# Branch A's attention values: two heads side by side as unsplit fp32 products of 64 columns, instead of split fp32r products of one head

## The chip, the cores and the metric

The kernel runs on one core of a Trainium2 chip. The metric is the device time of one execution in microseconds; a kernel is timed in several runs and the median is given. One execution was also taken by the hardware profiler: its page, its trace and the views of it are what this document reads. In them PE is TensorE's matmul stream, PEld its weight loads, DVE VectorE, ACT ScalarE, POOL GpSimd and SP SyncE, which issues the DMAs.

## What is computed

One encoder layer on two groups of 1024 rows of 1024 channels ("prompt" and "sample"), with the same weights. Branch A is grouped-query attention, and its last product is what the change edits:

```python
def gqa_attention(q, k, v):          # q: 8 heads of 64, k and v: 2 heads of 64
    s = jnp.einsum('bqgrd,bkgd->bgrqk', qblk, k).astype(jnp.float32) * scale
    p = jax.nn.softmax(s, axis=-1).astype(v.dtype)
    return jnp.einsum('bgrqk,bkgd->bqgrd', p, v)
```

Branch B is differential attention (4 heads, two softmax maps each, values of 128). Around them: one input projection to 5376 columns, gates, two branch projections, an output projection and a residual. All of it is in fp32.

## The kernel before

The kernel goes through the two groups one after the other. For each, the input projection is done by generators (`kva_gen`, `qa_gen`, `qkb_gen`, `vb_gen`, `z_gen`), each yielding after a few matmuls, and attention is a generator of steps too. `weave` draws from the streams in shares set by tables (`ATT_W`, `Z_SHARE`), and the framework then orders each engine's instructions by its own plan of the timeline, attention with higher priority. So on PE, products of the projections stand between those of attention. SP issues all DMAs in order.

Most products split their operands: a value x is kept as a rounded part xh (type fp32r) and the rest xl, and a product is the sum of two or three fp32r products.

Attention is cut into units of 256 queries. In branch A a unit is one head; there are 32 units per group, in two phases (the first and the second four q heads). A unit has two score steps (`scores`, `softmax_unit`): four products of 512 columns into a PSUM bank (L709, L710), the row maximum on DVE (L711), the exponential on ACT (L712). `flip` turns the probabilities: a block transpose on DVE (L745) and four DMAs into the tile q (L750). After that comes the values part, `a_values`:

- `pT_pieces` takes a quarter of the transposed probabilities at a time, ACT copies its rounded part to `hi` (L758), and DVE subtracts (L759), which leaves the low part in q.
- For each of 8 blocks of 128 keys PE makes two fp32r products of 256 columns: v times hi (L770), v times the low part (L771). The stationary operand has 128 columns: 64 of v's rounded part and 64 of its low part, so that the two halves of the accumulator hold two sums.
- ACT copies one half (L786), DVE adds the other (L787), a DMA stores 64 rows (L791).

Branch B's values (`b_values`, L810) are unsplit already: v and the probabilities in plain fp32, one product per block of keys with 128 stationary columns (the flag `WHOLE` is set for both pairs of heads). Each such product appears in the trace as two records. In the gates for the residual (L435) and at the start (L300) stand fp32 products with 2 stationary columns, and L889 transposes a tile of 64 columns. L497 and L679 are the products of the input projection (256 and 512 columns wide).

`attention` puts the steps of all units in one list, sorted by a number: unit n's score steps at n to n + 1, its values from n + `BEHIND` on.

Of the kernel before, what the change touches and what calls it, by code (L numbers as in the profile page):

```python
# [64 lines left out]
BEHIND = 1.4  # L65
AHEAD = 100
PV_LAG = 2

WHOLE = (True, True)
# [21 lines left out]
def kernel(ctx: ExitStack, tc: tile.TileContext, t: dict):  # L91
# [8 lines left out]
    qpool = ent(tc.tile_pool(name="qpool", bufs=2))  # L100
    tpool = ent(tc.tile_pool(name="tpool", bufs=2))
# [481 lines left out]
    def kva_gen(ht, out):  # L583
        w = kva_w.pop()[0] if kva_w else load_w(w_cols(w_in, (C_KA, 256)))
        k = v2(utile())
        va = utile().rearrange("p (n k d) -> p n k d", n=NTT, k=2)
# [58 lines left out]
    def vb_gen(ht, out, pr):  # L645
        w = load_w(w_cols(w_in, (C_VB + pr * 256, 256)))
        if WHOLE[pr]:
            v = utile().bitcast(F32).rearrange("p (n h e) -> p n h e", n=NTT, h=2)
            out[2 * pr], out[2 * pr + 1] = v[:, :, 0], v[:, :, 1]
        else:  # L650
            vs = [utile().rearrange("p (n s e) -> p n s e", n=NTT, s=2) for _ in range(2)]
            out[2 * pr], out[2 * pr + 1] = vs
        for tt in range(NTT):
            ps = yield from proj_tt(ht, w, tt)
            if WHOLE[pr]:
                nc.scalar.activation(v[:, tt].rearrange("p h e -> p (h e)"), ps, AF.Copy)
                yield 1
                continue
            for i in range(2):
                vp = ps[:, i * P : (i + 1) * P]  # L660
                nc.scalar.activation(vs[i][:, tt, 0, :], vp, AF.Copy)
                nc.vector.tensor_tensor(
                    out=vs[i][:, tt, 1, :], in0=vp, in1=vs[i][:, tt, 0, :].bitcast(F32), op=ALU.subtract
                )
            yield 1
# [51 lines left out]
    def scores(u, i):  # L717

        nm_ = len(u["q"])
        t, m = i // nm_, i % nm_  # L720
        qt = u["pr"] * 2 + t
        if "sw" not in u:
            u["sw"] = swapped(u)
        pt = ptile()
        su = u["su"][:, qt : qt + 1] if m == 0 else tiny.tile([P, 1], F32, tag="su", name=nm("su"))
        softmax_unit(u["q"][m][:, qt * P : (qt + 1) * P], u["sw"][:, m, t * P : (t + 1) * P], u["k"][m], pt, su)
        if m == 0:
# [8 lines left out]
        return t if m == nm_ - 1 else None  # L736

    def flip(u, t):


        pt = u[t][0]
        if len(u[t]) > 1:
            _, p1, f = u[t]
            nc.vector.scalar_tensor_tensor(out=pt, in0=p1, scalar=f, in1=pt, op0=ALU.mult, op1=ALU.add)
        nc.vector.transpose(pt, pt)  # L745
        if t == 0:
            u["pT"] = pair(F32R)
        dst = u["pT"].bitcast(F32).rearrange("p (i t f) -> p i t f", i=4, t=2)
        for i in range(4):
            dma(dst[:, i, t], pt[i * 32 : i * 32 + 32])  # L750

    def pT_pieces(u):

        pT = u["pT"].rearrange("p (q c b) -> p c q b", q=8, c=8)
        for cc in range(4):
            tl = pT[:, cc * 2 : cc * 2 + 2]
            th = tpool.tile([P, 2, 8, 32], F32R, tag="hi", name=nm("hi"), bufs=3)
            nc.scalar.activation(th, tl.bitcast(F32), AF.Copy)  # L758
            nc.vector.tensor_tensor(out=tl, in0=tl.bitcast(F32), in1=th.bitcast(F32), op=ALU.subtract)  # L759
            yield cc, th, tl  # L760

    def a_values(u):
        acc = ps_a.tile([P, 512], F32, tag="a", name=nm("a"))[:, :256]
        ready = []

        def pv(cc, th, tl):
            for c in range(2):
                k = cc * 2 + c
                lt = u["v"](k)
                nc.tensor.matmul(acc, lt, th[:, c, :], start=(k == 0), stop=False)  # L770
                nc.tensor.matmul(acc, lt, tl[:, c, :], start=False, stop=(k == 7))  # L771

        for piece in pT_pieces(u):
            ready.append(piece)
            if len(ready) > PV_LAG:
                pv(*ready.pop(0))
            yield 1
        while len(ready) > 1:
            pv(*ready.pop(0))
            yield 1  # L780
        pv(*ready.pop())
        tmp = mtile("at", [P, 256], bufs=1)
        o = mtile("oo", [P, 256])
        j = u["j"]
        a, b = (slice(0, 64), slice(64, 128)) if j % 2 == 0 else (slice(64, 128), slice(0, 64))
        nc.scalar.activation(tmp[a], acc[b], AF.Copy)  # L786
        nc.vector.tensor_tensor(  # L787
            out=query_order(o[a]), in0=piece_order(acc[a]), in1=piece_order(tmp[a]), op=ALU.add
        )
        pr = u["pr"]  # L790
        dma(u["od"][pr // 2][a, (pr % 2) * 256 : (pr % 2 + 1) * 256], o[a])  # L791
        yield 1

    def b_values(u):
        acc = ps_a.tile([P, 512], F32, tag="a", name=nm("a"))[:, :256]
        ready = []
        def pv(cc, th, tl):
            for c in range(2):
                k = cc * 2 + c
                for s, rt in ((0, th), (0, tl), (1, th)):  # L800
                    nc.tensor.matmul(
                        acc, u["v"][:, k, s, :], rt[:, c, :],
                        start=(k == 0 and s == 0 and rt is th), stop=(k == 7 and s == 1),
                    )

        if WHOLE[u["h"] // 2]:
            pT = u["pT"].bitcast(F32).rearrange("p (q c b) -> p c q b", q=8, c=8)
            yield 1
            for k in range(NCH):
                nc.tensor.matmul(acc, u["v"][:, k], pT[:, k], start=(k == 0), stop=(k == 7))  # L810
                if k % 2:
                    yield 1
        else:
            for piece in pT_pieces(u):
                ready.append(piece)
                if len(ready) > PV_LAG:
                    pv(*ready.pop(0))
                yield 1
            while len(ready) > 1:
                pv(*ready.pop(0))  # L820
                yield 1
            pv(*ready.pop())
# [20 lines left out]
    def attention(units):  # L843
# [11 lines left out]
        for at, ph, n, i, qk in steps:  # L855
# [4 lines left out]
            with tc.high_priority(offset=AHEAD):  # L860
# [12 lines left out]
                if t is not None:  # L873
                    late.append(lambda u=live[n], t=t: flip(u, t))
                    if t == (0 if ph < 2 else 0) and n + 1 < len(units) and units[n + 1][2]():
                        live[n + 1] = units[n + 1][1]()
                        late.append(lambda u=live[n + 1]: u.update(sw=swapped(u)))
# [138 lines left out]
    def units_of(st):  # L1016

        def a_unit(half, i, pr):
            j = half * 4 + i
            kv = j // 4  # L1020
            return {
                "q": [st["qa"][half][i % 2][:, i // 2]], "k": [st["ka"][:, kv]],
                "v": (lambda k: st["va"][:, k, kv, :]),
                "pr": pr, "j": j, "od": st["od"][j // 2], "su": st["suA"][:, j],
# [14 lines left out]
        for half in range(2):  # L1039
            units += [  # L1040
                (half, lambda a=(half, i, pr): a_unit(*a), lambda a=("qa", half, pr): there(*a))
                for i in (0, 2, 1, 3) for pr in range(4)
# [29 lines left out]
    for g in range(2):  # L1072
# [11 lines left out]
        def phase(k, *fs, more=()):  # L1084
            n_att = 16 * (6 + PV_LAG) if k < 2 else 4 * (9 + PV_LAG)
# [96 lines left out]
```

## Time and profile before

| | |
|---|---|
| runs (3): median, lowest, highest | 1982.26, 1980.13, 1987.66 us |
| the profiled execution, its span on the core | 1985.5 us |
| PE busy, records | 1908.6 us (96%), 10466 |
| DVE, ACT, POOL busy | 67%, 51%, 38% |
| branch A's products L770 + L771, records | 512 + 512 |
| branch A's attention runs in (us from the start) | about 150 to 550 and 1150 to 1560 |

A row of a group gives line, engine, operation, what is written from what, the shape (stationary rows*columns, then partitions x moving columns), the number, busy time and mean length of one in ns, then the engine's idle time just before and what ended it. A row of the timeline gives start, length over all, line and how many. Lengths of matmuls overlap, since the next starts before the last has ended: what one costs the stream is the distance of starts or ends.

### The profile page before, as it was taken

The numbers are of one execution on the slowest core, as the hardware profiler recorded it, in microseconds if no ns is written. First come the engines' busy times: TensorE is split into PE (matmuls) and PEld (weight loads), VectorE is DVE, ScalarE is ACT, GpSimd is POOL, SyncE is SP. The second block draws the span as 40 slices with busy tenths as digits, with TensorE's granted clock in tenths as the row PEclk, the third lists the DMA queues.
The fourth block names the chain that finished last, engine by engine and source line by source line (L and its number), as shares of the span: only waits on it lengthen the run. The fifth ranks groups of instructions, "written<-read, shape, count | busy, mean of one in ns | idle before, by whom it ended". The sixth has DMA issues, their size and how long they took to land.

```text
span 1985.5 us, 30670 instructions
## 1 busy us (share of the span) xinstructions
PE 1908.6 (96%) x10466; PEld 1627.8 (82%) x10466; DVE 1330.8 (67%) x1906; ACT 1009.9 (51%) x1939; POOL 758.1 (38%) x1008
## 2 busy tenths in 40 slices
PE   8889999999999998999999899999999999999999
PEld 3878888888878994778888787888887888877887
DVE  4558877777877577547465877677788845665641
ACT  4435655665654444754323565556655534566310
POOL 2374612453446252221235464134445626422110
PEclk9899999999999999999999999999999999999999
DMA  8124556555553345865641455565654333567532
GB/s 310 33 80 126 155 152 169 152 166 154 133 153 102 101 120 173 257 227 167 222 149 35 140 144 145 149 164 144 184 137 137 106 97 99 156 212 245 174 101 75
DMA packets 269531, 295.11 MB, mean 149 GB/s; under 512 B 35776, under 2 KB 218176, under 8 KB 269376
## 3 DMA queue, kind: packets, MB, share of 16 engines
q1 hardware_dynamic: 269376, 293.15, 49.7%
q8 instruction: 84, 1.38, 0.3%
q14 instruction: 71, 0.58, 0.1%
HBM read 133.59 MB, written 42.01 MB: 88 GB/s over the span
## 4 chain that ended last, share of the span: by engine, by line
PE 68%; DMA 8%; DVE 8%; ACT 5%; SPq 4%; issue 3%; POOL 3%; ACTq 0%; POOLq 0%; DVEq 0%
PE f L497 16%; PE f L679 16%; PE f L950 6%; PE f L979 5%; PE s L709 4%; PE a L810 4%; PE s L710 4%; PE s L979 4%; DMA q<-p 3%; SPq L750 3%; PE s L950 2%; DVE q L759 2%; PE a L771 2%; PE a L770 2%; DVE m L711 2%
## 5 line engine op out<-in xcount | busy, mean ns | idle before, releaser
L679 PE MATMUL f<-u,w 128*128 128x512 f32 x2232 | 582.3, 398 | 0.1
L497 PE MATMUL f<-w,u 128*128 128x256 f32 x3456 | 487.0, 286 | 2.2 <-ACT ev L685 1.4
L497 PEld LDWEIGHTS f<-w,u 128*128 128x128 f32 x3456 | 459.5, 192 | 22.4 <-ACT ev L685 1.8
L679 PEld LDWEIGHTS f<-u,w 128*128 128x128 f32 x2232 | 408.8, 190 | 77.3 <-POOL w L181 0.8
L181 POOL TENSOR_TENSOR w<-st,w 128x512 fp32r<-128x512 f32 x168 | 230.3, 1390 | 439.9 <-ACT w L179 375.1
L712 ACT ACTIVATE p<-s,m 128x1024 f32<-128x1024 f32 x256 | 284.4, 1111 | 206.3 <-DVE m L711 111.3
L711 DVE TENSOR_REDUCE m<-s 128x1 f32<-128x1024 f32 x256 | 310.0, 1216 | 51.3 <-PE s L710 48.7
L745 DVE STREAM_TRANSPOSE p<-p 128x1024 f32<-128x1024 f32 x192 | 238.2, 1241 | 99.2 <-ACT p L712 86.5
L759 DVE TENSOR_TENSOR q<-q,hi 128x512 fp32r<-128x512 f32 x256 | 198.3, 792 | 60.6 <-ACT hi L758 58.6
L515 POOL TENSOR_TENSOR rs<-ss,nhalf 128x4 f32<-128x4 f32 (+1 forms) x112 | 112.8, 1007 | 322.8 <-DVE ss L514 284.0
L758 ACT ACTIVATE hi<-q 128x512 fp32r<-128x512 f32 x256 | 153.8, 625 | 104.1 <-DMA q<-p 55.4
L710 PE MATMUL s<-u,sw 128*128 128x512 f32 x512 | 206.7, 404 | 0.0
L179 ACT ACTIVATE w<-st 128x512 fp32r<-128x512 f32 x196 | 113.9, 625 | 97.2 <-DMA st<-in_w_in_dram 46.0
L950 PE MATMUL f<-u,w 128*128 128x512 f32 x552 | 133.4, 395 | 5.1 <-ACT ev L685 4.4
L770 PE MATMUL a<-hi,u 128*128 128x256 f32 x512 | 132.5, 285 | 2.1 <-DVE oo L787 2.1
L771 PE MATMUL a<-q,u 128*128 128x256 f32 x512 | 129.8, 286 | 1.2 <-DVE q L759 1.2
L810 PE MATMUL a<-q,u 128*128 128x256 f32 x512 | 128.3, 390 | 1.9 <-DVE oo L826 1.5
L950 PEld LDWEIGHTS f<-u,w 128*128 128x128 f32 x552 | 103.9, 190 | 27.2 <-ACT ev L685 4.7
L709 PE MATMUL s<-u 128*128 128x512 f32 x256 | 110.9, 433 | 15.1 <-ACT p L712 15.1
L810 PEld LDWEIGHTS a<-q,u 128*128 128x128 f32 x512 | 97.8, 196 | 17.5 <-DVE oo L826 1.6
L709 PE MATMUL s<-u,u 128*128 128x512 f32 x256 | 103.6, 405 | 8.3 <-ACT p L712 7.7
L710 PEld LDWEIGHTS s<-u,sw 128*128 128x128 f32 x512 | 98.4, 192 | 15.5
(175 smaller groups left out, 2562.1 us busy)
## 6 DMA issues: line engine op xcount, KB each, us to landing
q<-p SPq DMA_DIRECT2D x768, 128.0 KB, 2.6
st<-in_w_in_dram SPq DMA_DIRECT2D x132, 256.0 KB, 3.0
zd<-ev SPq DMA_DIRECT2D x96, 256.0 KB, 2.2
sw<-u SPq DMA_DIRECT2D x256, 64.0 KB, 2.1
p<-zd SPq DMA_DIRECT2D x64, 256.0 KB, 3.2
u<-in_w_ada_dram SPq DMA_DIRECT2D x8, 1024.0 KB, 10.4
st<-in_w_in_dram SPq DMA_DIRECT2D x64, 128.0 KB, 2.7
st<-in_w_out_dram SPq DMA_DIRECT2D x32, 256.0 KB, 2.9
```

What stands on the lines that cost most here:

```text
L181: e.tensor_tensor(out=wl, in0=st, in1=wh.bitcast(F32), op=ALU.subtract)
L497: nc.tensor.matmul(ps, lt[c][:, sl], w[:, c, wi, :], start=(k == 0), stop=(k == 23))
L679: nc.tensor.matmul(ps, w[:, c, wi, e * P : (e + 1) * P], rt[c], start=(k == 0), stop=(k == 23),)
L709: nc.tensor.matmul(s[:, sl], q, k[:, sl], start=True, stop=False)
L710: nc.tensor.matmul(s[:, sl], sw, k[:, sl], start=False, stop=True)
L711: nc.vector.tensor_reduce(out=m, in_=s, axis=AX.X, op=ALU.max, negate=True)
L712: nc.scalar.activation(pt.rearrange("p (j c a) -> p j c a", j=4, c=8), s.rearrange("p (c a j) -> p j c a", c=8, j=4), AF.Exp, bias=m, accu ...
L745: nc.vector.transpose(pt, pt)
L759: nc.vector.tensor_tensor(out=tl, in0=tl.bitcast(F32), in1=th.bitcast(F32), op=ALU.subtract)
L810: nc.tensor.matmul(acc, u["v"][:, k], pT[:, k], start=(k == 0), stop=(k == 7))
L950: nc.tensor.matmul(ps, w[:, c, wi, d * P : (d + 1) * P], o[:, oi, :], start=(k == 0), stop=(k == 11))
L979: nc.tensor.matmul(ps, w[:, c, wi, e * P : (e + 1) * P], m[:, mi, :], start=(k == 0), stop=(k == 23))
```

## The change

Branch A's unit becomes a pair of heads that share k and v (16 units per group in place of 32). A pair has four score steps: both query tiles of the first head, then both of the second; each head has a tile q of its own for the transposed probabilities, and the pool of those grows from two to three. Nothing is split any more: v is kept in fp32 (64 columns per kv head), ACT's and DVE's splitting of the probabilities is gone, and `a_values` makes, per block of keys, one fp32 product of 256 columns for each head. The first head's goes to rows 0 to 63 of the accumulator, the second's to rows 64 to 127, each with 64 stationary columns. ACT then copies all 128 rows at once and one DMA stores them. A pair's value steps stand from n + 1.05 on and are 0.65 times as far apart (`PAIRS`). In branch B only code that was no longer reached is removed.

```diff
-    qpool = ent(tc.tile_pool(name="qpool", bufs=2))
-    tpool = ent(tc.tile_pool(name="tpool", bufs=2))
+    qpool = ent(tc.tile_pool(name="qpool", bufs=3))
...
-            vt = va[:, tt]
-            nc.scalar.activation(vt[:, :, 0:64], vp, AF.Copy)
-            nc.vector.tensor_tensor(out=vt[:, :, 64:128], in0=vp, in1=vt[:, :, 0:64].bitcast(F32), op=ALU.subtract)
+            nc.scalar.activation(va[:, tt], vp, AF.Copy)
...
-        nm_ = len(u["q"])
-        t, m = i // nm_, i % nm_
+        pairs = "h" not in u
+        t, m = (i % 2, i // 2) if pairs else (i // 2, i % 2)
...
     def a_values(u):
         acc = ps_a.tile([P, 512], F32, tag="a", name=nm("a"))[:, :256]
-        ready = []
-
-        def pv(cc, th, tl):
-            for c in range(2):
-                k = cc * 2 + c
-                lt = u["v"](k)
-                nc.tensor.matmul(acc, lt, th[:, c, :], start=(k == 0), stop=False)
-                nc.tensor.matmul(acc, lt, tl[:, c, :], start=False, stop=(k == 7))
-
-        for piece in pT_pieces(u):
-            ready.append(piece)
-            if len(ready) > PV_LAG:
-                pv(*ready.pop(0))
-            yield 1
...
-        nc.scalar.activation(tmp[a], acc[b], AF.Copy)
-        nc.vector.tensor_tensor(
-            out=query_order(o[a]), in0=piece_order(acc[a]), in1=piece_order(tmp[a]), op=ALU.add
-        )
+        pT = [x.rearrange("p (q c b) -> p c q b", q=8, c=8) for x in u["pT"]]
+        yield 1
+        for k in range(NCH):
+            for hd, rows in enumerate((LO, HI)):
+                nc.tensor.matmul(acc[rows], u["v"][:, k], pT[hd][:, k], start=(k == 0), stop=(k == 7))
+            if k % 2:
+                yield 1
         o = mtile("oo", [P, 256])
+        nc.scalar.activation(query_order(o), piece_order(acc), AF.Copy)
...
-            na, nv = (2, 4 + PV_LAG) if ph < 2 else (4, 5 + PV_LAG)
-            steps += [(n + i / na, ph, n, i, True) for i in range(na)]
-            steps += [(n + BEHIND + i / nv, ph, n, i, False) for i in range(nv)]
+            nv, behind, pace = (6, *PAIRS) if ph < 2 else (7, BEHIND, 1.0)
+            steps += [(n + i / 4, ph, n, i, True) for i in range(4)]
+            steps += [(n + behind + i * pace / nv, ph, n, i, False) for i in range(nv)]
```

In the changed kernel the lines move: L770 and L771 become L752, L810 becomes L766, L497 L494, L679 L661, L709 and L710 L691 and L692, L548 (transposes of q and k) L545.

On PE, the values of one head early in the first group stood like this before (a is the accumulator, hi and q the two parts of the probabilities, u the tile of v; numbers are buffers):

```order
L548 MATMUL f_1984<-ident,row_1636 128x128 x2
L770 MATMUL a_1787<-hi_1788,u_397 128x256
L771 MATMUL a_1787<-q_1665,u_397 128x256
L770 MATMUL a_1787<-hi_1788,u_397 128x256
L771 MATMUL a_1787<-q_1665,u_397 128x256
...
L771 MATMUL a_1787<-q_1665,u_397 128x256
L679 MATMUL f_2034<-u_283,w_2017 128x512
```

The first pair of heads there now, where q_1537 holds the first head's probabilities and q_1580 the second's:

```order
L661 MATMUL f_1493<-u_549,w_1335 128x512
L752 MATMUL a_1629<-q_1537,u_394 64x256
L691 MATMUL s_1647<-u_393,u_916 128x512
...
L661 MATMUL f_1493<-u_548,w_1335 128x512 x2
L752 MATMUL a_1629<-q_1580,u_394 64x256
L752 MATMUL a_1629<-q_1537,u_394 64x256
L752 MATMUL a_1629<-q_1580,u_394 64x256
...
L752 MATMUL a_1629<-q_1580,u_394 64x256
L691 MATMUL s_1758<-u_393,u_917 128x512
```

One product of the first head stands alone, 31 rows ahead of the rest, and the other 15 stand together, the heads in turn; before, both kinds of products had the whole width of 128.

In the second half of the first phase the values stand between products of the projection, here before:

```order
L497 MATMUL f_1868<-w_1435,u_283 128x256
L770 MATMUL a_1682<-hi_1730,u_397 128x256
L497 MATMUL f_1868<-w_1435,u_283 128x256
L497 MATMUL f_1868<-w_1435,u_284 128x256
L497 MATMUL f_1868<-w_1435,u_283 128x256 x2
L497 MATMUL f_1868<-w_1435,u_284 128x256
L771 MATMUL a_1682<-q_1573,u_397 128x256
```

and here with the change:

```order
L494 MATMUL f_2891<-w_2664,u_324 128x256 x2
L752 MATMUL a_3007<-q_2761,u_394 64x256
L494 MATMUL f_2891<-w_2664,u_325 128x256
L752 MATMUL a_3007<-q_2924,u_394 64x256
L661 MATMUL f_2910<-u_548,w_2732 128x512
L752 MATMUL a_3007<-q_2761,u_394 64x256
L661 MATMUL f_2910<-u_549,w_2732 128x512
L752 MATMUL a_3007<-q_2924,u_394 64x256
L661 MATMUL f_2910<-u_548,w_2732 128x512 x2
```

What moved: single 64-column products now alternate with 128-column ones. Over the whole program the 512 products stand in 148 unbroken stretches: 20 of 15 products, 108 of one, 20 of other lengths.

More of the change, by code (lines that the diff above doesn't have):

```diff
@@ L65 @@
 BEHIND = 1.4
+PAIRS = (1.05, 0.65)
 AHEAD = 100
-PV_LAG = 2
-WHOLE = (True, True)
 def weave(*streams):
@@ L646, in vb_gen @@
         w = load_w(w_cols(w_in, (C_VB + pr * 256, 256)))
[L647 to L652, printed above, removed]
+        v = utile().bitcast(F32).rearrange("p (n h e) -> p n h e", n=NTT, h=2)
+        out[2 * pr], out[2 * pr + 1] = v[:, :, 0], v[:, :, 1]
         for tt in range(NTT):
             ps = yield from proj_tt(ht, w, tt)
-            if WHOLE[pr]:
-                nc.scalar.activation(v[:, tt].rearrange("p h e -> p (h e)"), ps, AF.Copy)
-                yield 1
[L658 to L661, printed above, removed]
-                nc.vector.tensor_tensor(
-                    out=vs[i][:, tt, 1, :], in0=vp, in1=vs[i][:, tt, 0, :].bitcast(F32), op=ALU.subtract
-                )
+            nc.scalar.activation(v[:, tt].rearrange("p h e -> p (h e)"), ps, AF.Copy)
             yield 1
@@ L724, in scores @@
         pt = ptile()
-        su = u["su"][:, qt : qt + 1] if m == 0 else tiny.tile([P, 1], F32, tag="su", name=nm("su"))
+        if pairs:
+            su = u["su"][:, m, qt : qt + 1]
+        else:
+            su = u["su"][:, qt : qt + 1] if m == 0 else tiny.tile([P, 1], F32, tag="su", name=nm("su"))
         softmax_unit(u["q"][m][:, qt * P : (qt + 1) * P], u["sw"][:, m, t * P : (t + 1) * P], u["k"][m], pt, su)
+        if pairs:
+            u[m, t] = [pt]
+            return m, t
         if m == 0:
@@ L735, in scores, with flip @@
             u[t] += [pt, f]
[L736 to L743, printed above, removed]
+        return (0, t) if m else None
+    def flip(u, mt):
+        m, t = mt
+        if "h" in u:
+            mt = t
+        pt = u[mt][0]
+        if len(u[mt]) > 1:
+            _, p1, f = u[mt]
             nc.vector.scalar_tensor_tensor(out=pt, in0=p1, scalar=f, in1=pt, op0=ALU.mult, op1=ALU.add)
@@ L746, in flip @@
         if t == 0:
-            u["pT"] = pair(F32R)
-        dst = u["pT"].bitcast(F32).rearrange("p (i t f) -> p i t f", i=4, t=2)
+            pT = pair()
+            if "h" in u:
+                u["pT"] = pT
+            else:
+                u.setdefault("pT", []).append(pT)
+        dst = (u["pT"] if "h" in u else u["pT"][m]).rearrange("p (i t f) -> p i t f", i=4, t=2)
         for i in range(4):
             dma(dst[:, i, t], pt[i * 32 : i * 32 + 32])
[L752 to L760, printed above, removed]
@@ L795, in b_values @@
         acc = ps_a.tile([P, 512], F32, tag="a", name=nm("a"))[:, :256]
[L796 to L817, printed above, removed]
+        pT = u["pT"].rearrange("p (q c b) -> p c q b", q=8, c=8)
+        yield 1
+        for k in range(NCH):
+            nc.tensor.matmul(acc, u["v"][:, k], pT[:, k], start=(k == 0), stop=(k == 7))
+            if k % 2:
                 yield 1
[L819 to L822, printed above, removed]
         sq = mtile("at", [P, 256], bufs=1)
@@ L874, in attention @@
                     late.append(lambda u=live[n], t=t: flip(u, t))
-                    if t == (0 if ph < 2 else 0) and n + 1 < len(units) and units[n + 1][2]():
+                    if t == (0, 0) and n + 1 < len(units) and units[n + 1][2]():
                         live[n + 1] = units[n + 1][1]()
@@ L1016, in units_of, with a_unit @@
     def units_of(st):
-        def a_unit(half, i, pr):
-            j = half * 4 + i
-            kv = j // 4
+        def a_unit(half, b, pr):
+            kv = half
+            j = half * 4 + 2 * b
             return {
-                "q": [st["qa"][half][i % 2][:, i // 2]], "k": [st["ka"][:, kv]],
-                "v": (lambda k: st["va"][:, k, kv, :]),
-                "pr": pr, "j": j, "od": st["od"][j // 2], "su": st["suA"][:, j],
+                "q": [st["qa"][half][i][:, b] for i in range(2)], "k": [st["ka"][:, kv]] * 2,
+                "v": st["va"][:, :, kv, :],
+                "pr": pr, "od": st["od"][j // 2], "su": st["suA"][:, j : j + 2],
             }
@@ L1040, in units_of @@
             units += [
-                (half, lambda a=(half, i, pr): a_unit(*a), lambda a=("qa", half, pr): there(*a))
-                for i in (0, 2, 1, 3) for pr in range(4)
+                (half, lambda a=(half, b, pr): a_unit(*a), lambda a=("qa", half, pr): there(*a))
+                for b in range(2) for pr in range(4)
             ]
```

16 lines of the change are left out of this document (3 added, 13 removed).

## The prediction

> **What bounds the kernel now.** I read the page first, for how busy each engine is.
>
> ```profile
> span 1985.5 us, 30670 instructions
> ...
> PE 1908.6 (96%) x10466; PEld 1627.8 (82%) x10466; DVE 1330.8 (67%) x1906; ACT 1009.9 (51%) x1939; POOL 758.1 (38%) x1008
> ```
>
> The span is 1985.5 us; the runs shown lie on both sides of it (1980.13 to 1987.66, median 1982.26), so 3.2 us divide this execution from the median. TensorE (PE) is busy 96%. An average hides stages, so next come the two stretches in which branch A's attention runs, in the view by windows (times and counts: PE, PEld, DVE, ACT, POOL):
>
> ```profile
> 150.00:550.00 400.00, 397.38 (x2357) 350.25 (x2355) 308.25 (x398) 239.30 (x476) 164.12 (x210) 1.00 0.55 152
> ...
> 1150.00:1560.00 410.00, 398.66 (x2362) 352.80 (x2361) 311.77 (x411) 240.05 (x479) 173.10 (x235) 0.99 0.54 148
> ```
>
> There PE is busy 397 of 400 us and 399 of 410, DVE about 77%, ACT 60%, at the full granted clock (1.00, 0.99). A busy PE could still be one that waits inside its instructions, so the view of waits comes third: PE in the first of these stretches.
>
> ```profile
> PE s L709 <- ACT p L712: 1.4, 3, 1.0
> PE f L548 <- ACT ev L685: 0.3, 1, 0.3
> PE a L771 <- DVE q L759: 0.3, 1, 0.3
> PE f L497 <- ACT ev L685: 0.2, 1, 0.2
> PE s L709 <- DMA q<-p: 0.2, 1, 0.2
> ```
>
> All of it is 2.4 us in 400. **In the stage that the change edits, PE's own stream is the bound**: what ACT and DVE are spared there can give back those 2.4 us and no more, and what PE streams more or less goes into the end one for one.
>
> **What the products cost now.** The groups by shape:
>
> ```profile
> L770 PE MATMUL a<-hi,u 128*128 128x256 f32 x512 | 132.5, 285 | 2.1 <-DVE oo L787 2.1
> L771 PE MATMUL a<-q,u 128*128 128x256 f32 x512 | 129.8, 286 | 1.2 <-DVE q L759 1.2
> L810 PE MATMUL a<-q,u 128*128 128x256 f32 x512 | 128.3, 390 | 1.9 <-DVE oo L826 1.5 <-DMA q<-p 0.4
> ```
>
> The 285 ns of one is a latency: the next starts before it ends. What each takes of the stream is the distance of starts, from the timeline (start, length):
>
> ```profile
> 300.23 0.28 PE L770 MATMUL a<-hi,u 128*128 128x256 f32 x1
> ...
> 301.55 0.28 PE L771 MATMUL a<-q,u 128*128 128x256 f32 x1
> 301.67 1.84 PE L497 MATMUL f<-w,u 128*128 128x256 f32 x14
> ...
> 304.48 0.40 PE L710 MATMUL s<-u,sw 128*128 128x512 f32 x1
> 304.72 0.87 PE L497 MATMUL f<-w,u 128*128 128x256 f32 x6
> ...
> 703.02 1.02 PE L810 MATMUL a<-q,u 128*128 128x256 f32 x4
> ...
> L810 PE MATMUL a<-q,u x512: 377/379/634, 555.9 to 1811.9; 128*128 128x256 f32 x171
> ```
>
> From 300.23 to 301.67 stand 12 products of L770 and L771, so one takes 0.120 us. Removed: 1024 x 0.120 = **122.9 us**. L810 is the unsplit fp32 product of branch B: 256 instructions in the program, 512 records, so each is two records. A product of 512 columns takes 0.24 (L710 at 304.48, what follows it at 304.72). Four records of L810 last 1.02 us and the last of them 0.38 (the median, 379 ns, in the last row, which is from the view of that line), so one takes (1.02 - 0.38) / 3 = 0.213 us, and one product 0.427 us.
>
> **What they cost after.** Branch A then has 512 such products of 256 columns, 1024 records. No row shows a stationary operand of 64 columns in a product of this kind, so the first question is whether half the width costs less. The nearest row has 2 columns (moving 512 wide):
>
> ```profile
> 752.18 0.44 PE L548 MATMUL f<-ident,row 128*128 128x128 f32 x2
> 752.55 2.74 PE L435 MATMUL f<-st,cT 128*2 128x512 f32 x6
> 755.22 0.50 PE L709 MATMUL s<-u 128*128 128x512 f32 x1
> 755.55 0.40 PE L710 MATMUL s<-u,sw 128*128 128x512 f32 x1
> ...
> L435 PE MATMUL f<-st,cT 128*2 128x512 f32 x32 | 15.7, 609 | 2.5 <-DMA st<-in_w_ada_dram 2.5
> ```
>
> Six records last 2.74 us and one by itself 0.61 (the mean in the last row), so one takes (2.74 - 0.61) / 5 = 0.426 us, twice L810's 0.213 at twice the moving width. Narrow weights make nothing faster. What is left is whether two heads stream at once, each through its own half of the array:
>
> - *taking turns:* 1024 x 0.213 = 218.1 us;
> - *side by side:* a stretch of n alternating products needs n + 1 record times, since a product's second record can run beside the other head's first one. In the order of the changed kernel I count 148 stretches: 20 of 15 products, 108 of a single one, 20 of other lengths. That is (512 + 148) x 0.213 = **140.6 us**. If every record had a partner, 512 x 0.213 = 109.1 us would be the floor.
>
> I take 140.6: the 2-column row says that a product leaves unused columns idle for its whole time, and the change gives the two heads disjoint columns and disjoint output rows. It remains a choice, and both ends go into the range.
>
> **The price of changing the tile.** Each stretch puts a 64-column tile between 128-column ones. The same L435 rows show such a change at 2 columns. In: the two L548 end at 752.18 + 0.44 = 752.62, the six L435 at 752.55 + 2.74 = 755.29; between those ends lie 2.67 us, of which six records stream 6 x 0.426 = 2.56, so 0.11 is lost. Out: L710 ends at 755.95, 0.66 after L435; two products of 512 columns take 0.48, so 0.18 is lost. The weight load says why:
>
> ```profile
> 755.22 0.19 PEld L709 LDWEIGHTS s<-u 128*128 128x128 f32 x1 [0.86 <-DVE u L551]
> ```
>
> L709's weights are loaded from 755.22 on, when the last L435 (until 755.29) is all but over. But one row has 64 columns and no such loss, the transpose of L889:
>
> ```profile
> 1730.98 0.85 PE L679 MATMUL f<-u,w 128*128 128x512 f32 x3
> 1731.67 0.27 PE L889 MATMUL f<-ident,suA 128*64 128x128 f32 x1
> 1731.69 0.48 PE L679 MATMUL f<-u,w 128*128 128x512 f32 x1
> ...
> L889 PEld LDWEIGHTS f<-ident,suA 128*64 128x64 f32 x2 | 0.2, 109 | 0.9 <-issue 0.9
> L435 PEld LDWEIGHTS f<-st,cT 128*2 128x2 f32 x32 | 1.9, 83 | 10.6 <-DMA st<-in_w_ada_dram 6.2 <-issue 3.9 <-DMA tab<-rA 0.4
> ```
>
> It starts at 1731.67 while the L679 before it ends at 1731.83, and the next starts 0.02 later. So a round trip costs between 0 (L889) and 0.29 us (L435: 0.11 + 0.18), the latter with 109 - 83 = 26 ns more for the longer weight load: 0.32. I take **0.32**, since L889 is a transpose and L435 a product like the new ones: 148 x 0.32 = **47.4 us**; the range keeps 0.
>
> The Trainium skill, page "TensorEngine Tiling (Array Packing)", section "Key Properties", has a rule that speaks against this change: changing the tiling mode, unlike changing the tile within it, drains TensorE; it says also that different tiles can execute in parallel. By the rule the 47 us fall due; by the L889 row none would. The same page ("Restrictions and Gotchas") excludes transposes of fp32 from column tiling, by which L889 would never have changed the mode; L435 agrees with the rule, and no run here shows a 64-column product.
>
> **The rest of the change.** It goes off PE's path:
>
> ```profile
> L758 ACT ACTIVATE hi<-q 128x512 fp32r<-128x512 f32 x256 | 153.8, 625 | 104.1 <-DMA q<-p 55.4 <-PE a L770 42.5 <-PE s L710 1.9
> L786 ACT ACTIVATE at<-a 64x256 f32<-64x256 f32 x64 | 24.2, 378 | 1.5
> L759 DVE TENSOR_TENSOR q<-q,hi 128x512 fp32r<-128x512 f32 x256 | 198.3, 792 | 60.6 <-ACT hi L758 58.6 <-DMA zd<-ev 1.0
> L787 DVE TENSOR_TENSOR oo<-a,at 64x256 f32<-64x256 f32 x64 | 26.7, 418 | 1.1
> SPq L750 <- PE a L771: 32.1, 17, 3.5
> q<-p SPq DMA_DIRECT2D x768, 128.0 KB, 2.6
> ```
>
> ACT loses 153.8 + 24.2 us and gains 32 evictions (about 0.38 each as L786: 12 us), DVE loses 198.3 + 26.7, the subtraction of v's low part goes too, SP loses 32 issues of od. By the 2.4 us of waits above that is worth about nothing to the end. If PE were no longer the cover, ACT and DVE would be further from being the bound than now.
>
> A wait is moved: the first product of each pair now waits for the transposed probabilities' transfer itself (2.6 us to land) and no longer for DVE's subtraction, and behind it on PE stands all that follows, projections included. The order puts the pair's first product alone, ahead of the others, so the second head has a stage more to land. I take 0; if each of the 32 pairs lost 1 us it would be 32. On SP a transfer into q now waits for one of three buffers, of which a pair holds two; the row shows 32 us of such waits over the first A stretch already, without PE noticing, and behind them stand the loads of w's pieces. At nothing too.
>
> **Sum:** -122.9 + 140.6 + 47.4 = +65.1 us. On the profiled 1985.5 this is 2050.6; less the 3.2 us, about **2047 us**.
>
> **The rivals.**
>
> 1. *The two heads take turns* (no overlap, the change drains): -122.9 + 218.1 + 47.4 = +142.6, 2125 us. For it: every product of the trace runs alone in the array. Without the drain it would be +95.2, 2077 us.
> 2. *Not slower: changing the width costs nothing*, as at L889, and the halves overlap. Then the end lies between 109.1 - 122.9 = -13.8 and 140.6 - 122.9 = +17.7, by how many lone records find a partner: 1968 to 2000, middle 1984. It stays within 10 us of no change as long as streams and round trips together take under 122.9 + 10 us: with every record paired a round trip may then cost (132.9 - 109.1) / 148 = 0.16 us, and with none priced 24 us of records may go unpaired. Against it stands L435.
> 3. *PE waits for the transfers*: the 32 us above on top of the forecast, 2079.
>
> The change could also fail to do what it says if the halves never meet: that is rival 1.
>
> Page "TensorE: Matmul & The Clock Gate" of the Trainium skill, section "Part 3: Packing small matmuls — row/col tiling", gives 2.38 times for three column tiles. Taken as an estimate for two at the same efficiency (2.38 / 3 = 0.79), fully paired streams would take 109.1 / 0.79 = 138 us and the forecast would rise by 29, to 2076; no run here shows it.
>
> **How the numbers follow.** Forecast 0.38 (by itself 2030 to 2070). Taking turns with drain 0.16, without 0.06. No price for the width 0.35, of which 0.17 faster, 0.13 the same, 0.05 slower. Waits 0.05. What a measurement tells from no change is about 0.5%, 10 us: faster 0.17, same 0.13, slower 0.70. The range goes from the floor of rival 2 to just past rival 1: 1968 to 2130.
>
> **What would show it.** In the profile after, for L752: starts of records of the two heads 0.21 us apart with both running, two per step (overlap), or one per step (turns); the weight load behind a stretch starting only near its end (drain), or during it; PE's busy share in the A stretches staying near 97%, and these stretches together longer by about 65 us. I am wrong if the next 128-column product starts within 0.05 us of a stretch's end, if a run of 15 lasts 6.4 us and not 3.4, or if PE shows waits of tens of us for q<-p.

## The result and the profile after

The changed kernel takes 2038.29 us (median of 3 runs, 2037.57 to 2040.37) and the kernel before 1982.26: ratio 1.0273, 95% interval [1.0247, 1.0299], 56 us slower. The forecast was 2047 us in a range of 1968 to 2130.

The page of the profiled execution after (busy time, share of the span, count by engine):

```profile
span 2038.6 us, 29738 instructions
...
PE 1966.4 (96%) x10466; PEld 1581.8 (78%) x10466; DVE 1110.1 (54%) x1570; ACT 862.5 (42%) x1653; POOL 723.7 (35%) x1008
```

PE is as busy as before in share and 58 us longer in time, with the same number of records; DVE fell from 67% to 54% and ACT from 51% to 42%. The two stretches with branch A's attention, cut a little longer than before since the program is (same columns as before):

```profile
150.00:580.00 430.00, 430.00 (x2341) 327.62 (x2340) 214.67 (x246) 167.31 (x333) 141.90 (x206) 1.00 0.51 143
...
1185.00:1610.00 425.00, 423.93 (x2376) 332.03 (x2373) 218.62 (x270) 172.10 (x350) 161.90 (x239) 1.00 0.50 141
```

PE has 430 of 430 and 424 of 425 us, and about 2350 records took 425 to 430 us where before 2360 took 400 to 410. So the time went into PE's own stream and not into waits. The timeline shows how, with a product that stands alone and a stretch of 15 (start, length, line, number of records):

```profile
161.84 0.84 PE L661 MATMUL f<-u,w 128*128 128x512 f32 x3
162.62 0.65 PE L752 MATMUL a<-q,u 128*64 128x256 f32 x2
...
168.93 1.09 PE L661 MATMUL f<-u,w 128*128 128x512 f32 x4
169.96 3.67 PE L752 MATMUL a<-q,u 128*64 128x256 f32 x30
173.55 0.50 PE L691 MATMUL s<-u,u 128*128 128x512 f32 x1
173.89 0.39 PE L692 MATMUL s<-u,sw 128*128 128x512 f32 x1
174.12 0.39 PE L691 MATMUL s<-u,u 128*128 128x512 f32 x1
174.35 0.40 PE L692 MATMUL s<-u,sw 128*128 128x512 f32 x1
```

Ends are what to subtract. The lone product ends at 163.27 and the row before it at 162.68: 0.59 us for two records. The 15 products end at 173.63 and the row before them at 170.02: 3.61 us for 30 records. Thirty records one after the other would need 30 x 0.213 = 6.4 us; **the two heads do stream at once**. Call the time of one record, alone or beside one of the other head, a step. The lone product is two steps, the 15 are 16, so 14 steps more take 3.61 - 0.59 = 3.02 us, and one step 0.216. The starts in the trace say the same: in the stretch of 15 the records start two by two, some 7 ns apart, a pair every 0.216 us, and the last two alone, as 16 records of one head and 14 of the other would. Then 0.59 - 2 x 0.216 = 0.16 us is lost on the way into a stretch. On the way out L691 ends at 174.05, 0.42 after the stretch, where the next 512-column products follow each other in 0.23: 0.19 us is lost. The weight loads say the same:

```profile
169.95 3.21 PEld L752 LDWEIGHTS a<-q,u 128*64 128x64 f32 x30 [0.36 <-issue]
173.55 0.19 PEld L691 LDWEIGHTS s<-u,u 128*128 128x128 f32 x1 [0.38 <-issue]
```

The first load of the stretch starts at 169.95, 0.07 before the last 128-column product ends, and that of L691 at 173.55, 0.08 before the stretch ends; the load engine had stood idle 0.36 and 0.38 us before. By these rows both changes of the tile's width empty PE. This is the rule of the Trainium skill, page "TensorEngine Tiling (Array Packing)", section "Key Properties" (a change of mode drains, tiles work in parallel), and here the trace agrees with both halves of it.

The group rows: one by one the new records last about as long as those of branch B's products, which were L810 before (390 ns) and are L766 now.

```profile
L752 PE MATMUL a<-q,u 128*64 128x256 f32 x1024 | 172.0, 388 | 0.0
...
L766 PE MATMUL a<-q,u 128*128 128x256 f32 x512 | 131.9, 397 | 6.5 <-DMA q<-p 5.7
```

### The profile page after: what moved, and what is told of

It reads as the page before. It is cut to its first block, busy times and chain, and to the rows that moved or that the text cites. A ratio compares the mean times of both kernels' runs of the same rounds, so it can differ in the third digit from the quotient of the medians.

```text
span 2038.6 us, 29738 instructions
## 1 busy us (share of the span) xinstructions
PE 1966.4 (96%) x10466; PEld 1581.8 (78%) x10466; DVE 1110.1 (54%) x1570; ACT 862.5 (42%) x1653; POOL 723.7 (35%) x1008
## 4 chain that ended last, share of the span: by engine, by line
PE 80%; DMA 7%; DVE 4%; ACT 3%; POOL 2%; issue 2%; SPq 1%; ACTq 0%; POOLq 0%; DVEq 0%
PE f L661 22%; PE f L494 19%; PE a L752 8%; PE f L896 6%; PE s L691 5%; PE s L692 5%; PE a L766 4%; PE f L925 4%; PE s L896 2%; PE s L925 2%; DMA row<-zd 1%; POOL w L178 1%; DMA st<-in_w_in_dram 1%; PE f L545 1%; DMA p<-in_xT_sample_dram 1%
## 5 line engine op out<-in xcount | busy, mean ns | idle before, releaser
L661 PE MATMUL f<-u,w 128*128 128x512 f32 x2232 | 589.5, 401 | 3.5 <-ACT w L176 2.1
L494 PE MATMUL f<-w,u 128*128 128x256 f32 x3456 | 495.5, 286 | 2.3 <-ACT ev L667 1.6
L494 PEld LDWEIGHTS f<-w,u 128*128 128x128 f32 x3456 | 457.0, 191 | 44.8 <-issue 23.5
L661 PEld LDWEIGHTS f<-u,w 128*128 128x128 f32 x2232 | 410.5, 190 | 101.3 <-issue 18.5
L694 ACT ACTIVATE p<-s,m 128x1024 f32<-128x1024 f32 x256 | 285.1, 1114 | 249.3 <-DVE m L693 196.1
L178 POOL TENSOR_TENSOR w<-st,w 128x512 fp32r<-128x512 f32 x168 | 221.4, 1336 | 475.6 <-ACT w L176 445.1
L692 PE MATMUL s<-u,sw 128*128 128x512 f32 x512 | 205.2, 402 | 0.0
L752 PE MATMUL a<-q,u 128*64 128x256 f32 x1024 | 172.0, 388 | 0.0
L896 PE MATMUL f<-u,w 128*128 128x512 f32 x552 | 134.5, 397 | 3.9 <-DVE u L907 2.2
L766 PE MATMUL a<-q,u 128*128 128x256 f32 x512 | 131.9, 397 | 6.5 <-DMA q<-p 5.7
L691 PE MATMUL s<-u 128*128 128x512 f32 x256 | 110.6, 432 | 16.7 <-ACT p L694 16.7
L752 PEld LDWEIGHTS a<-q,u 128*64 128x64 f32 x1024 | 79.0, 136 | 59.7 <-issue 21.7
L548 DVE TENSOR_TENSOR u<-f,u 64x256 fp32r<-64x256 f32 (+1 forms) x196 | 80.5, 411 | 69.9 <-ACT u L547 64.8
L766 PEld LDWEIGHTS a<-q,u 128*128 128x128 f32 x512 | 99.9, 200 | 23.2 <-issue 5.9
L506 ACT ACTIVATE row<-f 128x256 f32<-128x256 f32 (+1 forms) x112 | 41.1, 367 | 175.6 <-PE f L494 164.7
L692 PEld LDWEIGHTS s<-u,sw 128*128 128x128 f32 x512 | 97.6, 191 | 18.9 <-issue 2.7
L691 PE MATMUL s<-u,u 128*128 128x512 f32 x256 | 104.3, 410 | 4.5 <-ACT p L694 3.7
```

The lines of the kernel that those rows point to most:

```text
L178: e.tensor_tensor(out=wl, in0=st, in1=wh.bitcast(F32), op=ALU.subtract)
L494: nc.tensor.matmul(ps, lt[c][:, sl], w[:, c, wi, :], start=(k == 0), stop=(k == 23))
L661: nc.tensor.matmul(ps, w[:, c, wi, e * P : (e + 1) * P], rt[c], start=(k == 0), stop=(k == 23),)
L691: nc.tensor.matmul(s[:, sl], q, k[:, sl], start=True, stop=False)
L692: nc.tensor.matmul(s[:, sl], sw, k[:, sl], start=False, stop=True)
L694: nc.scalar.activation(pt.rearrange("p (j c a) -> p j c a", j=4, c=8), s.rearrange("p (c a j) -> p j c a", c=8, j=4), AF.Exp, bias=m, accu ...
```

## The experiments

The theory: 0.216 us per step with the heads side by side, 0.16 in and 0.19 out per stretch, about 0.345 together in the finer numbers of the trace. The rivals: the loss is that of the longer fp32 products and the width costs nothing; the heads don't overlap; ACT's and DVE's load matters after all. Each expectation was written before its run. Medians are in us; "before" is the kernel before on the same chip.

### All products of a pair together

```diff
-        yield 1
-        for k in range(NCH):
-            for hd, rows in enumerate((LO, HI)):
-                nc.tensor.matmul(acc[rows], u["v"][:, k], pT[hd][:, k], start=(k == 0), stop=(k == 7))
-            if k % 2:
-                yield 1
+        for _ in range(4):
+            yield 1
+        with tc.high_priority(offset=3000):
+            for k in range(NCH):
+                for hd, rows in ((1, HI), (0, LO)):
+                    nc.tensor.matmul(acc[rows], u["v"][:, k], pT[hd][:, k], start=(k == 0), stop=(k == 7))
+        yield 1
```

> The changed kernel with all 16 products of a pair in one stretch (second head first, high priority): 32 stretches in place of 148. Theory (a record step 0.216 us, heads side by side, n + 1 steps in a stretch of n; each stretch 0.345 us for two changes of the tile): 544 x 0.216 + 32 x 0.345 = 128.5 us in place of 193.6, so 65 us less than the changed kernel: about 1973, level with the kernel before or a little faster. Rival 'the loss is fp32's own four passes, the changes of tile are free': only the 116 unpaired half steps go, 25 us, about 2013. Rival 'PE then waits for the transposed probabilities': 2038 or more, with waits of PE on DMA q<-p.

Measured: **1969.93**, ratio to before 0.9945 [0.9929, 0.9961]; later once more on another chip:

> e1_together once more on the same chip, as the measure for e7_dummy_free: 1970, ratio to the kernel before 0.9945.

1970.90, ratio 0.9939 [0.9920, 0.9959]. The timeline of one of its stretches:

```profile
184.04 1.12 PE L494 MATMUL f<-w,u 128*128 128x256 f32 x8
185.09 3.67 PE L754 MATMUL a<-q,u 128*64 128x256 f32 x32
188.69 0.74 PE L691 MATMUL s<-u,u 128*128 128x512 f32 x2
```

From end to end (185.16 to 188.76) it is 3.60 us for 32 records, no more than for 30. The same work in 32 stretches instead of 148 is 68 us faster than the changed kernel, by the theory's 65, and not by the rival's 25. The kernel with this edit is 12 us faster than the one before; some 4 of them may be the relief of ACT and DVE (below).

### The heads in turn, in 32 and in 155 stretches

The first edit's loops exchanged (heads outside, blocks of keys inside), with and without the high priority.

> As e1_together, but eight products of the second head, then eight of the first: same work, same 32 stretches, no neighbours on different halves except one. Theory (overlap needs neighbours on different halves): 992 steps x 0.216 + 32 x 0.345 = 225 us, 97 us more than e1_together: about 2070. Rival 'heads do not stream side by side, or PE reorders by itself': equal to e1_together.

> The heads in turn as in e2_in_turn_32, without the high priority, so 155 stretches in place of 32. Theory: nothing overlaps here anyway, so the difference to e2_in_turn_32 is the price of the changes alone: 123 x 0.345 = 42 us, plus up to 5 for lost neighbours: about 2115. Rival 'changes of tile are free': within 5 us of e2_in_turn_32.

Measured: 2056.45 (ratio 1.0390 [1.0359, 1.0420]) and 2106.23 (1.0632 [1.0597, 1.0667]). A stretch of the first:

```profile
188.02 1.24 PE L494 MATMUL f<-w,u 128*128 128x256 f32 x9
189.19 6.32 PE L754 MATMUL a<-q,u 128*64 128x256 f32 x32
195.44 0.73 PE L691 MATMUL s<-u,u 128*128 128x512 f32 x2
```

6.25 us from end to end (189.26 to 195.51) against 3.60: the order of the same 16 products decides whether they overlap. That is 86.5 us on the whole program; 97 were expected. (6.25 - 0.16) / 0.216 is 28 steps for 32 records, so at the border between the heads four records still found a partner, where I had counted one: in the trace the first head's first record starts 5 ns after the thirteenth of the second head's 16. The second kernel pays 49.8 us more for 123 more stretches, 0.40 each: the price of the changes (0.35) and some lost partners. Changes of width that cost nothing are out.

### No change of width, no overlap

```diff
-        acc = ps_a.tile([P, 512], F32, tag="a", name=nm("a"))[:, :256]
+        acc = ps_a.tile([P, 512], F32, tag="a", name=nm("a"))
+        acc = [acc[:, :256], acc[:, 256:]]
...
-        for k in range(NCH):
-            for hd, rows in enumerate((LO, HI)):
-                nc.tensor.matmul(acc[rows], u["v"][:, k], pT[hd][:, k], start=(k == 0), stop=(k == 7))
...
+        for hd in range(2):
+            for k in range(NCH):
+                nc.tensor.matmul(acc[hd], u["v"][:, k], pT[hd][:, k], start=(k == 0), stop=(k == 7))
...
-        nc.scalar.activation(query_order(o), piece_order(acc), AF.Copy)
+        src = (LO, HI)[u["kv"]]
+        for hd, rows in enumerate((LO, HI)):
+            nc.scalar.activation(query_order(o[rows]), piece_order(acc[hd][src]), AF.Copy)
...
-                "v": st["va"][:, :, kv, :],
+                "v": st["va"].rearrange("p n k d -> p n (k d)"), "kv": kv,
```

> Unsplit fp32 products with 128 stationary columns (both kv heads' values, of which one half is used), one head after the other into two column ranges of the bank: no change of tile, no overlap, and two evictions of 64 rows. Theory: 1024 x 0.216 = 221 us in place of 193.6: 27 us more than the changed kernel, about 2065. Rival 'the loss is fp32's own, narrow tiles bring and cost nothing': equal to the changed kernel, 2038. Rival 'the drains are most of the loss and the overlap is nothing': 51 us less, about 1987.

Measured: 2069.81, ratio 1.0454 [1.0429, 1.0480], near the theory's 2065. All of branch A's products have the full width there:

```profile
L753 PE MATMUL a<-q,u 128*128 128x256 f32 x1024 | 262.9, 379 | 0.0
```

Plain fp32 at full width is 31 us slower than the changed kernel and 100 slower than the first edit: narrow tiles win much when they stand together, and lose two thirds of that when they are scattered. The run also settles a rival that I had not named, that the price is one of changing between fp32r and plain fp32 and not of the width. Adding up over its trace each product's end less the end of the record ahead of it gives 221.3 us, 0.216 a record, though the products stand in 273 stretches among the fp32r ones, and a 512-column product behind a stretch ends 0.23 us after it, as anywhere else. Without a change of width nothing is lost on the way in or out.

### The first product alone again

The first edit with `enumerate((LO, HI))`: the first head's product is ready early and is issued alone, in 64 stretches.

> e1_together with the first head's product first again, so that one product of each pair stands alone and 15 together: 64 stretches. Theory: the lone one takes two record steps by itself (13.8 us in all) and 32 more stretches cost 0.345 each (11 us): 25 us more than e1_together, about 1995. The other 43 us of the changed kernel's loss against e1_together then belong to the stretches broken up by the projections. Rival 'the price is in the breaking up alone, the early lone product is paid by time in which PE would wait': equal to e1_together, 1970.

Measured: 1988.52, ratio 1.0028 [1.0013, 1.0043], 18.6 more than the first edit in place of 25. Adding up the ends in the same way over this trace and the first edit's, the stretches take 17.5 us more, and 32 more ways out, 0.197 us each in the changed kernel's trace on the mean, another 6.3: both terms are there. Why the time grew by 5 us less stays open. The changed kernel's 68 us over the first edit are thus 19 for the lone first product and 49 for stretches that the projections break up.

### What ACT's and DVE's relief is worth

The prediction gave it 2.4 us at most. First I put the load back into the first edit, as 512 copies on ACT and 512 subtractions on DVE that nothing reads.

```diff
+        for x in pT:
+            for c in range(NCH):
+                lo = mtile("at", [P, 256], bufs=1)
+                lo3 = lo.rearrange("p (q b) -> p q b", q=8)
+                nc.scalar.activation(lo3, x[:, c], AF.Copy)
+                nc.vector.tensor_tensor(out=lo3, in0=x[:, c], in1=lo3, op=ALU.subtract)
```

> e1_together with the splitting's load put back on ACT and DVE: for each head and block of keys ACT copies 256 columns of the transposed probabilities into a scratch tile and DVE subtracts it there (512 + 512 instructions, by the rows of 256-column copies about 0.38 and 0.42 us each, some 195 and 215 us); nobody reads the result, so this is extra work that the reference doesn't have. PE's 32 stretches stay. Theory (PE's stream is the bound, relief of ACT and DVE is worth the 2.4 us of waits at most): 1970 to 1975. Rival 'e1_together is faster than the kernel before because ACT and DVE are relieved': about 1982, ratio 1.00 to the kernel before.

Measured: 2123.43, ratio 1.0696 [1.0669, 1.0722]. The view of waits, ACT and then PE:

```profile
ACT at L753 <- DVE at L754: 229.9, 306, 2.6
```

```profile
PE s L691 <- ACT p L694: 97.2, 54, 6.1
```

My load was made badly: with one scratch tile ACT waits 230 us for DVE, the exponentials (L694) stand behind it, and PE waits 97 us for them. It says what a chain over one buffer costs and nothing of the load. So three more: two meant to be without that chain, the second of them also without a transfer to wait for, and a third meant to stand behind the exponentials in the queues:

```diff
+        sc = mtile("at", [P, 256], bufs=1).rearrange("p (q b) -> p q b", q=8)
+        o = mtile("oo", [P, 256])
+        o3 = o.rearrange("p (q b) -> p q b", q=8)
...
+                nc.scalar.activation(sc, pT[hd][:, k], AF.Copy)
+                nc.vector.tensor_tensor(out=o3, in0=pT[hd][:, k], in1=pT[hd][:, k], op=ALU.subtract)
...
+                nc.scalar.activation(sc, kk, AF.Copy)
+                nc.vector.tensor_tensor(out=o3, in0=kk, in1=kk, op=ALU.subtract)
...
+            if qk and ph < 2:
+                kk = live[n]["k"][0].bitcast(F32)[:, :256]
+                sc = mtile("at", [P, 256], bufs=1)
+                for _ in range(6):
+                    nc.scalar.activation(sc[:, :128], kk[:, :128], AF.Copy)
+                    nc.vector.tensor_tensor(out=sc[:, 128:], in0=kk[:, :128], in1=kk[:, :128], op=ALU.subtract)
```

> As e5_dummy_split (e1_together with the splitting's load put back on ACT and DVE, work that the reference doesn't have), but nothing of it waits for another engine: ACT copies each 256-column block into one scratch tile, DVE subtracts the block from itself into the tile that is overwritten by the eviction. 512 instructions of about 0.4 us on each engine. Theory (e5's loss came from ACT and DVE waiting for each other over one scratch tile, which held up the exponentials; the load itself is hidden under PE's stream): 1970 to 1980. Rival 'the load itself is what costs, so ACT's and DVE's relief is worth a good part of it': well above 1990.

> As e7_dummy_free (work that the reference doesn't have), but the 512 + 512 instructions read 256 columns of k, which have long been there, in place of the transposed probabilities: they can wait for no transfer. Theory (e7's 40 us came from ACT and DVE standing in their queues for the transfer of q, in front of the exponentials): back to 1970 to 1980. Rival 'the load itself costs': as e7, about 2010.

> As e8_dummy_k (extra work that the reference doesn't have, on k, waiting for no transfer), but at the priority of the projections and spread over the score steps, so that exponentials and maxima stand ahead of it in ACT's and DVE's queues: 768 copies and 768 subtractions of 128 columns, an estimate of 0.27 to 0.30 us each (rows of 128- and 256-column forms), some 210 to 230 us on each engine. Theory (load on ACT and DVE is hidden under PE's stream as long as it doesn't stand in front of what PE waits for): within 10 us of e1_together, 1970 to 1980. Rival 'the amount of load is what costs, wherever it stands': about 2010, as e7 and e8.

Measured: 2011.56 (1.0140 [1.0117, 1.0164]), 2015.57 (1.0157 [1.0130, 1.0185]), 2024.05 (1.0200 [1.0173, 1.0226]): 41 to 54 us over the first edit, all three on the rival's side. The group rows of the first of them, which are more than the splitting was (153.8 and 198.3 us):

```profile
L755 DVE TENSOR_TENSOR oo<-q 128x256 f32<-128x256 f32 x512 | 246.9, 496 | 76.9 <-DMA q<-p 50.7 <-DMA zd<-ev 6.0 <-DMA sw<-u 4.3
L754 ACT ACTIVATE at<-q 128x256 f32<-128x256 f32 x512 | 212.4, 415 | 110.9 <-DMA q<-p 75.0 <-DMA zd<-ev 10.0 <-DMA od<-oo 6.9
```

There ACT and DVE stand 75 and 51 us for the transfer of q. The other two loads weren't free of waits either. The second one's subtraction writes into the tile of the eviction, which an earlier store must leave first; the third one's copy and subtraction share one scratch tile again. DVE in the second, ACT in the third:

```profile
DVE oo L756 <- DMA od<-oo: 52.0, 15, 9.9
```

```profile
ACT at L829 <- DVE at L830: 57.1, 50, 3.2
```

PE's waits in the first edit, second run, and in the last of the three:

```profile
PE s L691 <- ACT p L694: 18.2, 12, 3.1
...
PE f L545 <- DVE row L534: 4.5, 2, 3.2
```

```profile
PE s L691 <- ACT p L694: 23.6, 21, 3.2
PE f L545 <- DVE row L534: 15.0, 5, 6.8
```

My theory, that the amount is hidden as long as it stands in front of nothing that PE waits for, did not come out; but since each load had waits of its own, the rival, that the amount alone costs, is not shown either. What can be said is where the time went. PE's idle time over the program (span less busy time on the page) is 69 us in the first edit and 98, 104 and 108 with the loads, and the mean granted clock is 0.978, 0.979 and 0.976 in place of 0.984, by span times the drop an estimate of 12, 10 and 16 us. Together that is 41, 45 and 55 us, about the whole loss (the profiled executions are 44, 46 and 55 us longer). The two rows above, PE's longer waits for the exponentials and for the rows that DVE prepares for q and k, are 16 of the 39 us of idle time in the last one. The test left to make was the opposite one, the relief where the change found the load: the kernel before with its splitting left out.

```diff
-            th = tpool.tile([P, 2, 8, 32], F32R, tag="hi", name=nm("hi"), bufs=3)
-            nc.scalar.activation(th, tl.bitcast(F32), AF.Copy)
-            nc.vector.tensor_tensor(out=tl, in0=tl.bitcast(F32), in1=th.bitcast(F32), op=ALU.subtract)
-            yield cc, th, tl
+            yield cc, tl, tl
```

> The kernel before without the splitting of branch A's probabilities: ACT's 256 copies (153.8 us) and DVE's 256 subtractions (198.3 us) are left out and both products of a block read the same unsplit tile, so the values come out doubled in their rounded part; PE's products, their shapes and number are those of before. It measures what the relief of ACT and DVE is worth where the change found them. Theory (PE's stream bounds these stages, PE's waits there are a few us): 1970 to 1982, ratio 0.994 to 1.00. Rival 'the relief is worth what the same load costs in e7 to e9, 41 to 53 us': about 1935, ratio 0.977.

Measured: 1977.21, ratio 0.9979 [0.9964, 0.9993]. There the relief of 154 us on ACT and 198 on DVE is worth 4 us (1 to 7). **In the old arrangement the load was nearly hidden; in the new one loads like it, each with waits of its own, were not.** The old splitting stood waiting too (104 us before L758 and 61 before L759 in the prediction's rows), so such waits by themselves don't tell the two apart. The windows don't explain it by the load's size. DVE and ACT in the first A stretch of the first edit (second run) and of the three loaded kernels in turn:

```profile
150.00:560.00 410.00, 407.65 (x2419) 335.97 (x2419) 224.61 (x259) 174.61 (x351) 153.73 (x215) 1.00 0.56 156
```

```profile
150.00:560.00 410.00, 392.44 (x2287) 323.08 (x2286) 318.41 (x491) 253.36 (x578) 147.20 (x198) 0.98 0.53 148
```

```profile
150.00:560.00 410.00, 398.78 (x2347) 327.56 (x2346) 309.11 (x471) 223.05 (x490) 151.37 (x205) 0.99 0.54 150
```

```profile
150.00:560.00 410.00, 394.05 (x2323) 323.65 (x2322) 307.13 (x530) 244.92 (x620) 144.02 (x203) 0.99 0.54 149
```

DVE is busy 307 to 318 of 410 us there, 75 to 78%, as in the kernel before (77%), and yet PE loses 9 to 15 us more to gaps than the first edit, at a granted clock of 0.98 or 0.99 in place of 1.00. What may differ is when the load comes and how the order around it was planned; the cause stays open. It does not bear on the verdict, since the changed kernel has no such load.

## Why the prediction was right

- **PE's stream as the bound:** held. PE fills the A stretches before and after, and the loss is in the stream. The two windows shown are together 45 us longer for about as many records (4719 before, 4717 after); about 65 were expected.
- **Half the columns make nothing faster:** held; the 64-column records last 379 ns in the median, as L810's, and a step is 0.216 us. The 0.213 read for L810 was 0.003 small: where its records stand together in the trace before, they start 0.216 apart.
- **The heads stream side by side:** the choice, for which no row before had a direct sign, held, shown by 3.60 against 6.25 us for the same 16 products. The rule was a little off: a stretch of n needs n + 1 steps for odd n, but n for even n (32 records took as long as 30), since the head with more products sets the number. Ten of these 148 stretches have an even n: ten steps, 2 us.
- **The price of a change, 0.32 us from the 2-column row:** 0.35 measured, and it was right to weigh the product L435 above the transpose L889. 148 x 0.35 = 52 us in place of 47.
- **What is removed, 122.9 us:** too small. Adding up over the trace before, for each of the 1024 products, its end less the end of the record ahead of it gives 129.2 us. Lone products take about 0.12 us there too; 3.3 us of the difference are PE's waits in front of some runs (2.1 and 1.2 in the group rows), and 1.5 are one run at 1221 us that went at a granted clock of 0.5.
- **The sum:** the same adding up gives 161.7 us for the new products, and 148 ways out at 0.197 another 29.2: 190.9 - 129.2 = +61.7, where +65.1 was forecast. The span grew by 53.1 and the median by 56.0. The rest, 6 to 9 us, came back elsewhere: PE's idle time over the program fell from 76.9 to 72.2 us, of which 3.3 are already counted with the old products, and the mean granted clock was 0.984 in place of 0.982, an estimate of some 4 us. What the relief is worth may lie in these. That the sum came so near owes something to luck: the removed term was 6 us too small and the new ones 3.
- **The relief, 2.4 us and no more:** too small. That list was of the first A stretch alone; in the second, from 1150 to 1560 us, PE's waits in the kernel before come to 11.3 us, of which the second, third and fifth row (5.8 us) wait for work of ACT and DVE in branch A's attention:

```profile
PE f L548 <- POOL row L537: 3.9, 1, 3.9
PE s L709 <- ACT p L712: 2.8, 5, 1.1
PE a L770 <- DVE oo L787: 2.1, 1, 2.1
PE f L548 <- ACT row L509: 1.6, 1, 1.6
PE a L771 <- DVE q L759: 0.9, 1, 0.9
```

The 4 us (1 to 7) of the last experiment are nearer to that.

- **The wait moved to the transfer:** taken at nothing, rightly. PE's own waits don't name L752; its weight loads show 1.0 us of waits for q<-p.
- **The rivals:** the heads in turn were out by the timeline. The one without a price for the width would have had 1968 to 2000, and the kernel that nearly fulfils it by having few changes takes 1970. The estimate of 0.79 that the prediction worked out from the Trainium skill's three-tile figure (page "TensorE: Matmul & The Clock Gate", "Part 3: Packing small matmuls — row/col tiling") does not show here: two tiles took 16 steps for 32 records, a factor of 2.0.

## What to carry to other kernels

Two half-width products side by side took the time of one here, but in these traces every change between half-width and full-width products emptied PE, and a round trip cost as much as 1.6 steps. So count the stretches in the order that the scheduler really makes before pricing such a change: the same products were 56 us slower in 148 stretches and 12 us faster in 32. Load that the profile shows as hidden gave 4 us when it was taken away, and 41 to 54 when something like it was put in at another place, for a reason that stays open; test both directions, and look in the trace of such a test for waits that the added load brings with it.

## What was not expected of the hardware

The overlap is complete: 32 records, two heads in turn by single products, took 16 steps of 0.216 us, as long as a record of L810 takes by itself in the full width. And with eight products of one head followed by eight of the other, 32 records took 28 steps and not 31.
